# Modulation weights in tiles of their own, and their pieces moved in a two-layer trunk kernel

## The chip, the cores and the metric

The kernel runs on one core of a Trainium2 chip. The metric is the device time of one execution in microseconds (us); the kernel before takes 2713.36 us, the median of 3 runs (2710.75 to 2714.07).

## What is computed

The reference is two layers of a trunk for 640 tokens of width 1024 (128 context tokens and 512 latent ones), all in fp32. Each layer is a half-step FFN, a token mixer, and a second half-step FFN. The scale, shift and gate of each of the three come from one matrix product with the condition, the modulation ("adaLN"):

```python
def adaln(cond, w, b):
    m = (jax.nn.silu(cond) @ w + b).reshape(cond.shape[0], 1, N_MOD, D_MODEL)
    return [m[:, :, j] for j in range(N_MOD)]
...
def ffn_branch(x, mods, g_pre, g_post, w_in, w_out):
    shift, scale, gate = mods
    y = swiglu(modulate(x, g_pre, shift, scale), w_in, w_out)
    return x + FFN_RES * gate * rmsnorm(y, g_post)
...
    for i in range(DEPTH):
        m_ctx = adaln(c_ctx[None, :], mod_w[i], mod_b[i])
        m_lat = adaln(c, mod_w[i], mod_b[i])
        xc = ffn_branch(xc, m_ctx[0:3], norm_pre[i, 0], norm_post[i, 0], ffn_w_in[i, 0], ffn_w_out[i, 0])
...
        if i % 2 == 0:
...
            yc, s_ctx, ckv_ctx, krope_ctx = even_mixer(hc, *w, s0, None, None)
...
            yc, s_ctx = odd_mixer(hc, *w, s0)
```

The condition has two rows only (context and latent), but `mod_w` is 1024 x 9216 per layer: 75.5 MB for two layers, read once. The Even mixer (layer 0) is a gated DeltaNet with 4 heads (a chunked scan whose chunks need the inverse of a triangular matrix) beside an attention with 4 heads ("MLA"); the Odd mixer (layer 1) is a chunked gated linear attention. Two FFNs per layer have a hidden width of 2816.

## The kernel before

**Stages.** The program runs FFN1, Even mixer, FFN2 (layer 0), then FFN1, Odd mixer, FFN2 (layer 1), and stores. The 640 tokens are five tiles of 128. An FFN goes over 22 tiles of 128 hidden columns, t = 0 to 21: TensorE computes t's hidden columns (L650, 320 tokens wide), and the product with `w_out` (L298, 512 wide) of earlier tiles follows in between. Every product is taken as three products of a high and a low half of its operands. The halves of a weight are made on ScalarE (hi, L603 and L182) and VectorE (lo, L604 and L183) from a raw tile of 512 KB that SP's queue has loaded (L591, L196, L201). Behind an FFN's loop stand `half_a` and `half_b` (L810 to L822): the last output products, the norm, the gate and the residual for tiles 0 to 2, then for 3 and 4, and the next stage's normalisation and transposes (L257).

**Pools.** Tiles come from pools with a fixed number of buffers; an instruction that writes a tile waits until the tile that held its buffer has been read for the last time. Raw weights, the modulation weights `mw`, the modulation bias `mb` and the two gate tiles `gb` of a sub-layer all share the pool `rawp`, 7 buffers.

**Modulation.** `adaln` (L364) is a generator of 80 pieces, numbered 0 to 79 here: 2 layers x 5 column blocks x 8 slices of 128 rows (`kc`). A piece loads two `mw` tiles (blocks 0 to 3) or one (block 4) on SP's queue (L376). At every odd `kc` the matmuls of the last two pieces are issued (L395): a **flush**, with 8 matmuls of 32 x 512 over four column groups (16 records in the trace), or 4 matmuls over two groups in block 4 (8 records). After the eighth piece the bias is added (L403), the block is transposed (L407) and copied to `modF` (L413), or a gate is written to DRAM.

**Where pieces stand.** The program calls for a piece (`filler`) at places that tables set: FILLS gives for each FFN how many pieces stand in its loop (one per t, L802) and how many in `half_b` (L821); the Even mixer has calls behind its projections, two `self.fill(2)` (L1606, L1612), and MFILL, a count for each of the seven steps of each of four attention heads (L1595). In the Even mixer `mla_head(0)` runs together with what the scheduler can place beside it: `gdn_inverse(1)` (L1191), `gdn_levels` (L1225) and `gdn_chain(1)` (L1299) of the second pair of DeltaNet heads, mostly VectorE and ScalarE work with 128-wide matmuls between. Pieces 30 to 60 fall into the Even mixer, 61 to 70 into the loop of layer 0's FFN2, 71 to 76 into its `half_b`, and 77 to 79 into the loop of layer 1's FFN1.

**Order.** A scheduler at build time orders the instructions of each engine and gives out the buffers; at run time each engine and SP's queue goes through its list strictly in that order. A matmul of a flush whose `mw` has not landed holds up all of TensorE, and a load whose buffer is not free holds up all loads behind it.

Of the kernel before, what the change touches and what calls it, by code (L numbers as in the profile page):

```python
# [9 lines left out]
F32 = mybir.dt.float32  # L10
# [4 lines left out]
ALU = mybir.AluOpType  # L15
# [3 lines left out]
P = 128  # L19
# [3 lines left out]
KC = 8  # L23
# [4 lines left out]
HW = (6400, 4096)  # L28
HT = TOK // 2
PLAIN = 2  # L30
FILLS = (((16, 6), (10, 6)), ((18, 0), (0, 0)))
EARLY = 5
SLOTS = ((2, 3, 4, 5, 6), (0, 1, 2, 3, 4))
TW = 648
MFILL = ((1, 1, 1, 1, 1, 1, 0), (1, 1, 1, 1, 1, 1, 0), (1, 0, 1, 0, 1, 0, 0), (0, 0, 0, 0, 0, 0, 0))
NH = 4
KQ = 4
GLA_LEVELS = (1, 2, 4, 8, 16, 32, 64)
# [32 lines left out]
class Ring:  # L71


    def __init__(self, bufs):
        self.bufs, self.n = list(bufs), 0
# [6 lines left out]
class Trunk:  # L82
    def __init__(self, ctx, tc, cf, cm):
        self.tc, self.nc, self.n = tc, tc.nc, 0
        nc = self.nc
        mk = lambda name, bufs, **k: ctx.enter_context(tc.tile_pool(name=name, bufs=bufs, **k))
        self.cst = mk("cst", 1)
        self.hp = mk("hp", 1)
        self.xp = mk("xp", 5)
        self.rawp = mk("rawp", 7)  # L90
        self.hlp = mk("hlp", 16)
        self.Tp = mk("Tp", 18)
        self.sml = mk("sml", 2)
        self.ps_up = mk("ps_up", 3, space=PSUM)
        self.ps_dn = mk("ps_dn", 2, space=PSUM)
        self.ps_pt = mk("ps_pt", 2, space=PSUM)
        self.ps_ad = mk("ps_ad", 1, space=PSUM)
        self.dram = mk("drm", 1, space=bass.MemoryType.DRAM)
        self.ident = self.cst.tile([P, P], F32, name="ident")
        make_identity(nc, self.ident)  # L100
        self.ones = self.cst.tile([P, P], F32, name="ones")
        nc.vector.memset(self.ones, 1.0)
        self.mhalf = self.cst.tile([P, 1], F32, name="mhalf")
        nc.vector.memset(self.mhalf, -0.5)
        self.onec = self.cst.tile([P, 1], F32, name="onec")
        nc.vector.memset(self.onec, 1.0)
        self.cf = self.cst.tile([P, CTOT], F32, name="cf")
        self.cm = self.cst.tile([P, 8, P], U8, name="cm")
        self.neg = self.cst.tile([P, 2, P], BF16, name="neg")
        self.cm_in, self.cf_in = cm, cf  # L110
        self.x = [None] * NT
        self.h = [None, None]
        self.look = False
# [232 lines left out]
    def cond_setup(self, c, c_ctx, norm_pre):  # L346
        nc = self.nc
        t = self.raw("crow")
        nc.sync.dma_start(t[0:8, 0:P], c_ctx.rearrange("(k p) -> k p", p=P))
        nc.sync.dma_start(t[8:16, 0:P], c[0].rearrange("(k p) -> k p", p=P))  # L350
        nc.sync.dma_start(t[64:112, 0:P], norm_pre.rearrange("l n (k p) -> (l n k) p", p=P))
        ps = self.pt()
        nc.tensor.transpose(ps[:, 0:16], t[0:16, 0:P], self.ident[0:16, 0:16])
        ps2 = self.pt()
        nc.tensor.transpose(ps2[:, 0:48], t[64:112, 0:P], self.ident[64:112, 64:112])
        self.cT = self.cst.tile([P, KC, 32], F32, name="cT")
        nc.vector.memset(self.cT, 0.0)
        nc.scalar.activation(self.cT[:, :, 0:2].rearrange("p k r -> p r k"), ps[:, 0:16].rearrange("p (r k) -> p r k", r=2), AF.Silu)
        self.gpre = self.cst.tile([P, 48], F32, name="gpre")
        nc.vector.tensor_copy(self.gpre, ps2[:, 0:48])  # L360
        self.modF = [self.cst.tile([P, 9, 2, KC], F32, name=f"modF{l}") for l in range(2)]
        self.gate_dr = [[self.dram.tile([2, D], F32, name=f"gate{l}_{n}") for n in range(3)] for l in range(2)]

    def adaln(self, mod_w, mod_b, norm_post):  # L364


        nc = self.nc
# [3 lines left out]
        def load():  # L371
            for l, q, kc in order:
                wt = []
                for half in range(2 if q < 4 else 1):
                    w = self.W(name="mw") if (l, q) == (0, 0) else self.raw("mw")
                    nc.sync.dma_start(w, mod_w[l, kc * P:(kc + 1) * P, q * 2048 + half * 1024:q * 2048 + half * 1024 + 1024])  # L376
                    wt.append(w)
                ready.append(wt)
                return

        for l in range(2):
            for q in range(5):
# [25 lines left out]
                for mi in range(nj // 2):  # L408
                    n = 2 * q + mi
                    if n % 3 < 2:  # L410
                        for r in range(2):
                            src = pt.rearrange("p (c m j r) -> p c m j r", c=4, m=2, j=2)[:, :, mi, :, r]
                            nc.vector.tensor_copy(self.modF[l][:, n, r].rearrange("p (j c) -> p c j", c=4), src)  # L413
                    else:
                        o = 64 * mi
                        g = norm_post[l, n // 3]
                        nc.scalar.dma_start(mb[o:o + 64, 512:1024], bass.AP(g.tensor, g.offset, [[512, 2], [0, 32], [1, 512]]))
                        nc.vector.scalar_tensor_tensor(mb[o:o + 64, 0:512], mb[o:o + 64, 0:512], 1.0 if n // 3 == 1 else 0.5, mb[o:o + 64, 512:1024], ALU.mult, ALU.mult)
                        for j in range(2):
                            nc.scalar.dma_start(self.gate_dr[l][n // 3][:, j * 512:j * 512 + 512], mb[o + 32 * j:o + 32 * j + 2, 0:512])  # L420
                yield True

    def scale_shift(self, l, n):
        nc = self.nc
        A = self.cst.tile([P, 2, KC], F32, name=f"A{l}_{n}")
        g = self.gpre[:, (l * 3 + n) * 8:(l * 3 + n) * 8 + 8]
        for s in range(2):
            nc.vector.scalar_tensor_tensor(A[:, s], self.modF[l][:, 3 * n + 1, s], 1.0, g, ALU.add, ALU.mult)
        return A, self.modF[l][:, 3 * n]

    def gate_rows(self, l, n):
        out = []
# [460 lines left out]
class Even(Mixer):  # L893
# [87 lines left out]
    def run(self, nxt):  # L981
        T, nc, i = self.T, self.T.nc, self.i
# [3 lines left out]
        k, q, vtok, vpad = ([None] * NH for _ in range(4))  # L986
# [204 lines left out]
        def gdn_inverse(pair, st, ering):  # L1191
# [27 lines left out]
            for s in range(4):  # L1219
# [2 lines left out]
                    nc.vector.tensor_copy(U3[r, :, 32 * s:32 * s + 32], u3[r, u0:u0 + n])  # L1222
                for c in range(NT):
                    nc.scalar.copy(v4(st.D[c])[r, :, 32 * s:32 * s + 32], d3[r, 4 * c:4 * c + 4])
        def gdn_levels(st):  # L1225
            for lv in (4, 5):
                mask = T.cm[:, lv].unsqueeze(1).to_broadcast([P, 4, P])
                for c in range(NT):
                    a, uu, dd = st.A[c], st.U[c], st.D[c]
                    py, pz = misc(), misc()  # L1230
                    for u in range(4):
                        nc.tensor.matmul(un(py, u), lhsT=un(a, u), rhs=un(dd, u), start=True, stop=True)
                    Y = ering()
# [10 lines left out]
            for c in range(NT):  # L1244
                a, uu, dd = st.A[c], st.U[c], st.D[c]
                py, pz, Y = misc(), misc(), ering()
                for u in range(4):
                    r, k = where[u % 2]
# [4 lines left out]
                for u in range(4):  # L1253
                    r, k = where[u % 2]
# [44 lines left out]
        def gdn_chain(pair, st):  # L1299
# [28 lines left out]
                        square(h, 0)  # L1328

            for t in range(4):  # L1330
                if t == 2:
                    context()
                cu = (1 + t, 4 - t)
# [136 lines left out]
        st1 = gdn_store(1)  # L1470
# [132 lines left out]
                        gens.remove(g)  # L1603

        one = (mb, hq, prs, pTs)
        self.fill(2)  # L1606
        mla_values()
        together(mla_head(0, *one))
        gdn_inverse(1, st1, ering)
        early = [gdn_out(0)]  # L1610
        gdn_levels(st1)
        self.fill(2)  # L1612
        gdn_chain(1, st1)
        w_out = i["ev_w_out"][0]
        ar = T.arena(1)
# [476 lines left out]
```

## Time and profile before

| | us |
|---|---|
| median of 3 runs | 2713.36 |
| the profiled execution, its time | 2716.26 |
| its span | 2714.5 |
| TensorE matmul busy (PE) | 2632.5 (97%) |
| TensorE weight loads busy (PEld) | 2331.2 (86%) |
| VectorE busy (DVE) | 1943.0 (72%) |
| ScalarE busy (ACT) | 1179.1 (43%) |
| mean DMA rate | 114 GB/s |

PE is the engine that multiplies, PEld its weight loads, which run beside the multiplying; matmuls overlap in their pipeline, so that the records of neighbours overlap too and PE shows as busy where it could have taken more. The steps of the next sections are read from stretches of the trace, given in us from the start of the span. In the profiled execution the Even mixer lies from about 500 to 1000, layer 0's FFN2 from there to about 1470, and layer 1's FFN1 behind it.

### The profile page before, as it was taken

The page shows a single profiled execution, that of the slowest core. Times are in us where ns is not written, and L with a number is a line of the kernel's source. Part 1 is how long each engine was busy: PE and PEld are TensorE (multiplying, and loading weights), DVE is VectorE, ACT ScalarE, POOL GpSimd, SP SyncE. Part 2 cuts the span into 40 slices and gives each one's busy share as a digit, 9 for nine tenths or more (in the row PEclk, how much of TensorE's full clock was granted, in tenths as well). Part 3 has the DMA queues.
Part 4 walks back from the last instruction along what each step waited for, and adds up shares of the span by engine and source line. Part 5 has one row for each costly group of instructions (what it writes and reads, how often), then busy time and mean ns, then how long its engine had stood idle before and what let it go on. Part 6 is the DMA issues. An engine that isn't in the chain of part 4 may idle for free. (4 is left out here: it accounts for less than half of the span.)

```text
span 2714.5 us, 41232 instructions
## 1 busy us (share of the span) xinstructions
PE 2632.5 (97%) x16040; PEld 2331.2 (86%) x16040; DVE 1943.0 (72%) x3731; ACT 1179.1 (43%) x2281; POOL 125.5 (5%) x301
## 2 busy tenths in 40 slices
PE   6999999999999999999999999999999999999998
PEld 4988888789858678888997999999899988999997
DVE  5777777768585558777778777777675749777776
ACT  5433333554345645332335433334765447333333
POOL 0000000200100010000001000000200002000001
PEclk8999999999999999999999999999999999999999
DMA  8334424734151334343227322224212143332222
GB/s 272 123 115 141 148 96 133 251 103 142 50 188 46 128 117 130 114 138 103 86 71 244 104 87 86 86 81 135 92 55 67 59 140 109 95 92 86 78 70 101
DMA packets 297099, 309.60 MB, mean 114 GB/s; under 512 B 13573, under 2 KB 250639, under 8 KB 296903
## 3 DMA queue, kind: packets, MB, share of 16 engines
q1 hardware_dynamic: 278240, 260.05, 30.1%
q10 hardware_dynamic: 18663, 46.92, 4.9%
q8 instruction: 126, 2.06, 0.3%
q14 instruction: 70, 0.57, 0.1%
HBM read 286.59 MB, written 20.33 MB: 113 GB/s over the span
## 5 line engine op out<-in xcount | busy, mean ns | idle before, releaser
L650 PE MATMUL up<-ar,hi 128*128 128x320 f32 x2944 | 658.6, 311 | 10.5 <-ACT ar L513 4.5
L650 PEld LDWEIGHTS up<-ar,hi 128*128 128x128 f32 x2944 | 502.4, 189 | 37.2 <-ACT ar L513 6.1
L650 PE MATMUL up<-ar,lo 128*128 128x320 f32 x1472 | 455.5, 310 | 0.6 <-DVE lo L604 0.6
L603 ACT CAST hi<-raw 128x1024 fp32r<-128x1024 f32 x256 | 268.1, 1050 | 295.4 <-PE up L650 258.4
L304 DVE TENSOR_TENSOR y<-y,dn 128x512 f32<-128x512 f32 x388 | 264.5, 682 | 151.9 <-PE dn L298 150.8
L604 DVE TENSOR_TENSOR lo<-raw,hi 128x1024 fp32r<-128x1024 f32 x256 | 312.4, 1222 | 75.1 <-ACT hi L603 74.5
L298 PE MATMUL dn<-hi,al 128*128 128x512 f32 x880 | 347.8, 395 | 0.1
L298 PE MATMUL dn<-lo,ah 128*128 128x512 f32 x880 | 347.6, 395 | 0.0
L298 PE MATMUL dn<-hi,ah 128*128 128x512 f32 x880 | 346.8, 395 | 0.7 <-DVE y L304 0.5
L650 PE MATMUL up<-hq,hi 128*128 128x320 f32 x1408 | 315.1, 310 | 0.3 <-DVE xn L707 0.3
L650 PEld LDWEIGHTS up<-ar,lo 128*128 128x128 f32 x1472 | 277.9, 189 | 1.3 <-DVE lo L604 1.3
L208 PE MATMUL up<-ar,hi 128*128 128x384 f32 (+1 forms) x1184 | 267.3, 315 | 4.9 <-ACT ar L274 4.0
L650 PEld LDWEIGHTS up<-hq,hi 128*128 128x128 f32 x1408 | 238.8, 188 | 21.5 <-issue 9.2
L650 PE MATMUL up<-hq,lo 128*128 128x320 f32 x704 | 217.4, 309 | 0.0
L208 PEld LDWEIGHTS up<-ar,hi 128*128 128x128 f32 x1184 | 200.6, 191 | 15.3 <-issue 5.6
L183 DVE TENSOR_TENSOR lo<-raw,hi 128x1024 fp32r<-128x1024 f32 x145 | 175.8, 1218 | 45.0 <-ACT hi L182 38.2
L298 PEld LDWEIGHTS dn<-hi,al 128*128 128x128 f32 x880 | 165.3, 188 | 39.3 <-DVE al L691 1.2
L298 PEld LDWEIGHTS dn<-hi,ah 128*128 128x128 f32 x880 | 165.2, 188 | 26.3 <-DVE y L304 1.4
L208 PE MATMUL up<-ar,lo 128*128 128x384 f32 (+1 forms) x592 | 184.3, 311 | 0.0
L298 PEld LDWEIGHTS dn<-lo,ah 128*128 128x128 f32 x880 | 165.1, 188 | 22.2
L182 ACT CAST hi<-raw 128x1024 fp32r<-128x1024 f32 x145 | 150.9, 1048 | 44.5 <-PE up L208 19.0
L658 ACT COPY h<-up 128x320 f32<-128x320 f32 x68 | 29.0, 426 | 314.3 <-PE up L650 314.3
(704 smaller groups left out, 4216.2 us busy)
## 6 DMA issues: line engine op xcount, KB each, us to landing
raw<-in_ffn_w_in_dram SPq DMA_DIRECT2D x188, 512.0 KB
mw<-in_mod_w_dram SPq DMA_DIRECT2D x144, 512.0 KB
raw<-in_ffn_w_out_dram SPq DMA_DIRECT2D x88, 512.0 KB
xdr<-x ACTq DMA_DIRECT2D x25, 512.0 KB
x<-xdr ACTq DMA_DIRECT2D x25, 512.0 KB
raw<-in_od_w_in_dram SPq DMA_DIRECT2D x24, 512.0 KB
raw<-in_ev_w_in_dram SPq DMA_DIRECT2D x19, 512.0 KB
gb<-gate ACTq DMA_DIRECT2D x12, 512.0 KB
```

The lines of the kernel that those rows point to most:

```text
L182: nc.scalar.copy(hi, raw)
L183: nc.vector.tensor_sub(lo, raw, hi.bitcast(F32))
L208: self.nc.tensor.matmul(ps[:, :n], lhsT=wt[a][:, kc], rhs=self.h[g][:, b, kc], start=k == 0, stop=k == 3 * KC - 1)
L298: nc.tensor.matmul(ps, lhsT=a(i, m), rhs=w[j][:, nh * 512:nh * 512 + 512], start=k == 0, stop=k == last)
L304: nc.vector.tensor_add(yd, yd, ps)
L603: nc.scalar.copy(hi, raw[:, :n])
L604: nc.vector.tensor_sub(lo, raw[:, :n], hi.bitcast(F32))
L650: nc.tensor.matmul(ps[:, :HT], lhsT=w[i][:, kc], rhs=b[j].at(kc), start=first and n == 0, stop=n == 11, skip_group_check=not first)
L658: self.T.nc.scalar.copy(p1, X[:, :HT])
```

## The change

It does five things. `mw` tiles get a pool of 4 buffers, and `rawp` goes from 7 to 4. FILLS moves the six pieces of `half_b` behind layer 0's FFN2 into its loop. MFILL of attention head 0 goes from 6 pieces to 3, and the two `fill(2)` go; in their place `gdn_levels` of the second pair takes one piece at odd c (4 pieces), and each of the two `gdn_chain` one at t = 0 and 2 (4 pieces). `modF` keeps 6 rows in place of 9. A DMA scratch area shrinks from 1024 to 256 bytes. Pieces 30 to 61 now fall into the Even mixer, 62 to 77 into the loop of FFN2, none into its `half_b`, and 78 and 79 into the next loop.

```diff
-FILLS = (((16, 6), (10, 6)), ((18, 0), (0, 0)))
+FILLS = (((16, 6), (16, 0)), ((18, 0), (0, 0)))
...
-MFILL = ((1, 1, 1, 1, 1, 1, 0), (1, 1, 1, 1, 1, 1, 0), (1, 0, 1, 0, 1, 0, 0), (0, 0, 0, 0, 0, 0, 0))
+MFILL = ((1, 0, 1, 0, 1, 0, 0), (1, 1, 1, 1, 1, 1, 0), (1, 0, 1, 0, 1, 0, 0), (0, 0, 0, 0, 0, 0, 0))
...
-        self.rawp = mk("rawp", 7)
+        self.rawp = mk("rawp", 4)
+        self.mwp = mk("mwp", 4)
...
-        self.modF = [self.cst.tile([P, 9, 2, KC], F32, name=f"modF{l}") for l in range(2)]
+        self.modF = [self.cst.tile([P, 6, 2, KC], F32, name=f"modF{l}") for l in range(2)]
...
-                    w = self.W(name="mw") if (l, q) == (0, 0) else self.raw("mw")
+                    w = self.W(name="mw") if (l, q) == (0, 0) else self.mwp.tile([P, 1024], F32, tag="mw", name=self.u("mw"))
...
-        def gdn_levels(st):
+        def gdn_levels(st, fill=0):
...
                     py, pz = misc(), misc()
+                    if c % 2:
+                        self.fill(fill)
...
             for t in range(4):
+                if t % 2 == 0:
+                    self.fill(1)
                 if t == 2:
                     context()
...
         one = (mb, hq, prs, pTs)
-        self.fill(2)
         mla_values()
         together(mla_head(0, *one))
         gdn_inverse(1, st1, ering)
         early = [gdn_out(0)]
-        gdn_levels(st1)
-        self.fill(2)
+        gdn_levels(st1, 1)
         gdn_chain(1, st1)
...
-    nc = bacc.Bacc("TRN2", target_bir_lowering=False, num_devices=1, dynamic_dma_scratch_size=1024)
+    nc = bacc.Bacc("TRN2", target_bir_lowering=False, num_devices=1, dynamic_dma_scratch_size=256)
```

**TensorE behind layer 0's FFN2.** The first matmuls of the next FFN (L650, L651 after the change, since lines shift by one) and the flushes around them; `up` and `dn` are the products' accumulators, `ad` that of the modulation. Before:

```order
L257 MATMUL pt_13622<-ident,xn_13603 128x128 x4
L395 MATMUL ad_10645<-mw_13695,cT 32x512
L395 MATMUL ad_10645<-mw_13697,cT 32x512 x2
L650 MATMUL up_13862<-ar_13346,hi_13495 128x320
L650 MATMUL up_13888<-ar_13346,hi_13501 128x320
L650 MATMUL up_13862<-ar_13346,hi_13495 128x320
L650 MATMUL up_13862<-ar_13346,lo_13496 128x320
L407 MATMUL pt_13710<-ident,mb_13707 128x128 x4
L395 MATMUL ad_13719<-mw_13720,cT 32x512 x2
L395 MATMUL ad_13719<-mw_13722,cT 32x512 x2
L395 MATMUL ad_13719<-mw_13728,cT 32x512 x2
L395 MATMUL ad_13719<-mw_13730,cT 32x512 x2
```

With the change:

```order
L258 MATMUL pt_13674<-ident,xn_13655 128x128 x4
L299 MATMUL dn_13733<-hi_13323,al_13300 128x512
L396 MATMUL ad_11923<-mw_14419,cT 32x512
L396 MATMUL ad_11923<-mw_14571,cT 32x512 x2
L651 MATMUL up_13871<-ar_13398,hi_13547 128x320
L651 MATMUL up_13897<-ar_13398,hi_13553 128x320
L651 MATMUL up_13924<-ar_13398,hi_13559 128x320
L651 MATMUL up_13871<-ar_13398,hi_13547 128x320
L651 MATMUL up_13871<-ar_13398,lo_13548 128x320
```

The transposes and the two flushes that stood behind the first four matmuls of the next FFN are gone; the last flush of all (pieces 78 and 79), which the program calls for in the next loop, has been placed ahead of them, and that loop holds none any more.

**TensorE in the Even mixer.** Attention head 0 before, its scores, transposes and products with the values (L1546, L1568, L1575, L1579, L1584), with flushes in pieces between them:

```order
L1546 MATMUL up_6648<-kr_6645,hq_7267 128x320
L395 MATMUL ad_7524<-mw_8241,cT 32x512
L1584 MATMUL up_6647<-ident,pr_7268 128x128
L395 MATMUL ad_7524<-mw_8241,cT 32x512
L395 MATMUL ad_7524<-mw_8243,cT 32x512 x2
L1568 MATMUL up_6647<-ident,pr_7269 128x128 x4
L395 MATMUL ad_7524<-mw_8270,cT 32x512
L1575 MATMUL up_6648<-ident,pr_7269 128x128
```

With the change flushes stand in `gdn_levels` of the second pair (L1235 to L1242):

```order
L1239 MATMUL dn_4821<-ar_7163,E_5418 128x128 x4
L396 MATMUL ad_7775<-mw_7721,cT 32x512
L1242 MATMUL pt_4824<-ident,ar_7163 128x128 x4
L1239 MATMUL pt_4823<-ar_7163,E_5419 128x128 x4
L1235 MATMUL pt_4824<-ar_7164,ar_7163 128x128 x4
L1242 MATMUL dn_4822<-ident,ar_7163 128x128 x4
L396 MATMUL ad_7775<-mw_7721,cT 32x512
L396 MATMUL ad_7775<-mw_7723,cT 32x512 x2
L396 MATMUL ad_7775<-mw_7776,cT 32x512
```

Flushes that stood between the steps of the attention head now stand between the level products, three of them by the end of the levels.

**SP's queue between layer 0's FFN1 and the Even mixer.** `ev_w_in` is the mixer's projection weight. Before:

```order
L376 DMA mw_4667<-in_mod_w_dram 128x1024
L376 DMA mw_4669<-in_mod_w_dram 128x1024
L376 DMA mw_4671<-in_mod_w_dram 128x1024
L376 DMA mw_4673<-in_mod_w_dram 128x1024
L376 DMA mw_4683<-in_mod_w_dram 128x1024
L376 DMA mw_4685<-in_mod_w_dram 128x1024
L376 DMA mw_4687<-in_mod_w_dram 128x1024
L376 DMA mw_4689<-in_mod_w_dram 128x1024
L196 DMA raw_4837<-in_ev_w_in_dram 128x8x128
L196 DMA raw_4843<-in_ev_w_in_dram 128x8x128
L196 DMA raw_4966<-in_ev_w_in_dram 128x8x128
```

With the change:

```order
L197 DMA raw_4840<-in_ev_w_in_dram 128x8x128
L197 DMA raw_4846<-in_ev_w_in_dram 128x8x128
L197 DMA raw_4969<-in_ev_w_in_dram 128x8x128
L197 DMA raw_5039<-in_ev_w_in_dram 128x8x128
L197 DMA raw_5109<-in_ev_w_in_dram 128x8x128
L377 DMA mw_4670<-in_mod_w_dram 128x1024
L377 DMA mw_4672<-in_mod_w_dram 128x1024
L377 DMA mw_4674<-in_mod_w_dram 128x1024
L377 DMA mw_4676<-in_mod_w_dram 128x1024
L377 DMA mw_4686<-in_mod_w_dram 128x1024
```

The eight `mw` loads of the second and third flush there now stand behind five loads of projection weights, and each waits until TensorE has used up a tile of the flush before.

## Rows read from the trace of the kernel before

**Rows 1.** The page: span, busy time of each engine.

```profile
span 2714.5 us, 41232 instructions
PE 2632.5 (97%) x16040; PEld 2331.2 (86%) x16040; DVE 1943.0 (72%) x3731; ACT 1179.1 (43%) x2281; POOL 125.5 (5%) x301
```

**Rows 2.** Windows: stretch, its length, busy us (records) of each engine, clock, DMA share, GB/s.

```profile
510.00:530.00 20.00, 18.36 (x96) 11.03 (x92) 10.39 (x20) 9.27 (x22) 4.08 (x15) 1.00 1.06 358
785.00:815.00 30.00, 27.90 (x154) 15.04 (x152) 25.37 (x138) 14.70 (x39) 0.00 (x0) 1.00 0.65 235
815.00:850.00 35.00, 34.33 (x260) 30.17 (x259) 16.16 (x33) 21.19 (x57) 0.00 (x0) 1.00 0.09 34
1100.00:1430.00 330.00, 329.94 (x1970) 300.17 (x1970) 247.88 (x371) 109.70 (x151) 0.00 (x0) 1.00 0.34 107
```

**Rows 3.** Timeline of PE in FFN2's loop: start, length, instruction.

```profile
1112.22 1.92 PE L395 MATMUL ad<-mw,cT 128*32 128x512 f32 x16
1114.08 0.56 PE L650 MATMUL up<-hq,hi 128*128 128x320 f32 x2
```

**Rows 4.** Timeline of PE behind FFN2, [idle before <- what ended it].

```profile
1458.23 1.90 PE L395 MATMUL ad<-mw,cT 128*32 128x512 f32 x10
...
1467.60 1.06 PE L395 MATMUL ad<-mw,cT 128*32 128x512 f32 x6
1470.94 0.81 PE L650 MATMUL up<-ar,hi 128*128 128x320 f32 x3 [2.29 <-ACT ar L513]
1472.58 5.32 PE L395 MATMUL ad<-mw,cT 128*32 128x512 f32 x16
1477.83 0.56 PE L650 MATMUL up<-ar,hi 128*128 128x320 f32 x2
```

**Rows 5.** Timeline of DVE there: the last operand of the next FFN's first half.

```profile
1472.53 0.49 DVE L514 TENSOR_TENSOR ar<-f,ar 128x192 fp32r<-128x192 f32 x2
```

**Rows 6.** Timeline of SP there.

```profile
1459.32 10.16 SPq L376 DMA_DIRECT2D mw<-in_mod_w_dram  x5
1472.68 8.14 SPq L591 DMA_DIRECT2D raw<-in_ffn_w_in_dram  x5
```

**Rows 7.** Timeline of PE in layer 1's FFN1.

```profile
1498.54 1.04 PE L395 MATMUL ad<-mw,cT 128*32 128x512 f32 x2
...
1534.88 1.90 PE L395 MATMUL ad<-mw,cT 128*32 128x512 f32 x6
1536.71 0.56 PE L650 MATMUL up<-hq,hi 128*128 128x320 f32 x2
...
1570.20 1.91 PE L395 MATMUL ad<-mw,cT 128*32 128x512 f32 x8
```

**Rows 8.** Windows of line 395 alone: busy us (records) of PE and PEld.

```profile
785.00:815.00 30.00, 9.51 (x48) 1.34 (x48) 1.00 0.65 235
815.00:850.00 35.00, 0.00 (x0) 0.00 (x0) 1.00 0.09 34
```

**Rows 9.** DVE's waits from 765 to 960: us in total, times, longest.

```profile
DVE mx L1547 <- PE up L1546: 10.4, 13, 1.4
```

**Rows 10.** SP's waits over the whole span.

```profile
SPq L591 <- DVE lo L604: 701.0, 85, 32.4
SPq L376 <- PE ad L395: 221.7, 32, 29.0
```

**Rows 11.** Timeline of PE between FFN1 and the Even mixer.

```profile
507.50 2.78 PE L395 MATMUL ad<-mw,cT 128*32 128x512 f32 x24
...
512.09 1.05 PE L395 MATMUL ad<-mw,cT 128*32 128x512 f32 x4
...
524.14 0.44 PE L257 MATMUL pt<-ident,xn 128*128 128x128 f32 x2 [1.24 <-ACT h L239]
```

**Rows 12.** Timeline of SP there.

```profile
512.11 15.09 SPq L196 DMA_DIRECT2D raw<-in_ev_w_in_dram  x6
```

**Rows 13.** Timeline of DVE there: the last product with a gate tile.

```profile
510.01 0.68 DVE L281 TENSOR_TENSOR y<-y,gb 128x512 f32<-128x512 f32 x1
```

More of the change, by code (lines that the diff above doesn't have):

```diff
@@ L412, in adaln @@
                             src = pt.rearrange("p (c m j r) -> p c m j r", c=4, m=2, j=2)[:, :, mi, :, r]
-                            nc.vector.tensor_copy(self.modF[l][:, n, r].rearrange("p (j c) -> p c j", c=4), src)
+                            nc.vector.tensor_copy(self.modF[l][:, n - n // 3, r].rearrange("p (j c) -> p c j", c=4), src)
                     else:
@@ L427, in scale_shift @@
         for s in range(2):
-            nc.vector.scalar_tensor_tensor(A[:, s], self.modF[l][:, 3 * n + 1, s], 1.0, g, ALU.add, ALU.mult)
-        return A, self.modF[l][:, 3 * n]
+            nc.vector.scalar_tensor_tensor(A[:, s], self.modF[l][:, 2 * n + 1, s], 1.0, g, ALU.add, ALU.mult)
+        return A, self.modF[l][:, 2 * n]
     def gate_rows(self, l, n):
```

## The prediction

> **What bounds the kernel.** I read the page first, then the windows, then the timelines at the places that the diff touches. The page shows TensorE busy for 2632.5 of 2714.5 us and nothing else above 72% [rows 1]; so a change pays only where TensorE waits, or where it does work that could be done in a wait. The windows tell the two kinds of place apart. In the loop of layer 0's FFN2 PE is busy for 329.94 of 330 us and its weight loads for 300.17 [rows 2]: there is no wait, and whatever is put in is paid in full. In the Even mixer from 785 to 815, with attention head 0, PE shows 27.90 of 30 but PEld only 15.04, while DVE has 25.37: matmul records overlap there without the array being full, VectorE sets the pace, and a matmul put between costs little. From 815 to 850, where the second pair's chain follows, PEld is at 30.17 of 35 and DVE at 16.16 [rows 2]: PE is nearly full again. The same 80 pieces are computed before and after; the change only moves 40 flushes about. The reader is to see that it moves some from places where PE waits to places where it does not, and others the other way.
>
> **The price of a flush.** In the FFN2 loop a flush of 16 records begins at 1112.22 and the next matmul at 1114.08: 1.86 us [rows 3]. In layer 1's FFN1 a flush of 8 records, two column groups in place of four, takes from 1534.88 to 1536.71: 1.83 us [rows 7]. So half the work costs the same, and I take 1.85 us for either kind where PE is saturated.
>
> **Term 1, the loop of layer 0's FFN2.** Before, four flushes stand there, up to piece 69; with the change seven, up to piece 77. Three more at 1.85 us in a stretch without idle time: **+5.6 us**. A flush there has no cover, so below 5 us it can't be.
>
> **Term 2, behind layer 0's FFN2.** Three flushes stood here. The first was in two parts: one, of 1.90 us, stood among the output products at 1458.23, and I take 1.8 us for it; the other, at 1467.60, lies in a wait of 2.29 us that ends only when ScalarE has the next FFN's operand at 1470.94, and costs nothing [rows 4]. The other two came as 16 records of 5.32 us at 1472.58, and the next matmul of the FFN starts at 1477.83 [rows 4]. What these matmuls need was there when VectorE ended the last `ar` at 1472.53 + 0.49 = 1473.0 [rows 5], so 4.8 us of this are delay. They took 5.3 us in place of 3.7 in a stretch where SP issued five `mw` loads over 10 us and the next weights only from 1472.68 [rows 6], so part was waiting for data. All of it goes: 1.8 + 4.8 = **-6.6 us**. The bound on the other side: if the next weights are late once this delay is gone (they are issued at 1472.68 now), only the 1.8 us stay. I take nearly the whole, because SP no longer has `mw` loads ahead of those weights and the first tile's weights are split before 1473. The last flush (pieces 78, 79) now stands right ahead of the next FFN's first matmul, in the place of the one at 1467.60: the wait of 2.29 us hides it, 0 to +1.9 us; I take **0**.
>
> **Term 3, layer 1's FFN1.** The two flushes that stood in its loop (2 + 6 and 8 records) go: 0.97 us for the small part (1498.54 to about 1499.5), 1.83 and, for the 8 records of 1.91 us at 1570.20, 1.84 [rows 7]: **-4.6 us**, in a loop as full as FFN2's.
>
> **Term 4, the Even mixer.** It takes one flush more. From 785 to 815 48 records of L395, three flushes, lay between attention head 0's steps, and from 815 to 850 none [rows 8]. With the change three stand in the second pair's levels, where PE is nearly full, so up to 3 x 1.85 = 5.6 us that were hidden come out, and the added flush may cost 1.85 more: at most +7.4. Against it, VectorE waited 10.4 us for scores of attention over the heads [rows 9], and flushes ahead of those scores are part of that; with half of head 0's pieces gone some of it returns: -4 us at best. From the weight-load share I take 50% of the exposed 5.6 us, 2.8, and of the added one 0.5, less 2: **+1.3 us**, with -4 and +7.4 as ends. Here a rule speaks against the move. The Trainium skill ("Trainium Kernel Development and Optimization", Best Practices) says to judge how near TensorE is to its limit by the busy share of its weight loads and not of its matmuls; by matmul share head 0 (93%) and the levels (98%) look alike and term 4 would be only the added flush, about +2; by the weight loads (50% and 86%) head 0 has room and the levels don't, and it would be up to +7. No row decides it; the rows of VectorE make me stay between.
>
> **Term 5, the pools.** Four raw buffers in place of seven: in an FFN a t needs three raw loads, and SP already spent 701 us waiting for buffers of that kind [rows 10], which cost PE nothing in the saturated loops; I take 0 there. Two gate tiles hold two of the four at each stage's end, where the next weights may come later by the 3 us of two tiles at 358 GB/s [rows 2]: 0 to +3 us; **+0.5**. The `mw` pool of four is just one flush: the next flush's loads wait for PE to use up the last, and PE releases them already in 221.7 us of waits now [rows 10]. That matters only where flushes follow closely, between FFN1 and the Even mixer, where a flush and a half run at 507.50 and the next parts from 512.09 on [rows 11]. There the next four tiles can no longer be loaded early, but their place in the transfers goes to projection weights, which before were issued from 512.11 on [rows 12], and the stretch from 510 to 530 moved 358 GB/s at a DMA share of 1.06 [rows 2]: total bytes bound it, and these are the same. 0 to +7 (worked out below), **+1**.
>
> The smaller `modF` and scratch area change no instruction: 0. I know of no row in which a DMA needs that area.
>
> **The sum.** 5.6 - 6.6 - 4.6 + 1.3 + 0.5 + 1 = -2.8. Against the profiled execution, 2716.3, this gives 2713.5; that execution lies 2.9 above the median of 2713.4, so against the runs it is 2710.6. Predicted: **2710.5 us**. About 0.2%, 5.4 us, is what a measurement of this kernel can tell from no change: below 2708.0 is faster, above 2718.8 slower.
>
> **The rivals.**
> *A, the mixer gains (faster).* If VectorE's chain of head 0 and the inverse beside it is what ends the mixer's middle, and the flushes moved into the levels fill short waits of PE there for ScalarE and VectorE, term 4 is -4 and not +1.3: 2705. For it: DVE at 25.37 of 30 us and the 10.4 us of waits [rows 2, 9]. Against it: 30.17 of 35 us of weight loads in the levels' stretch.
> *B, `mw` starves (slower).* Between FFN1 and the mixer the four tiles of the next flush are behind five projection loads in SP's queue, and the last of these waits for a buffer that a gate tile holds until its last product ends at 510.69 [rows 13]. Then the first `mw` is issued near 511 and four tiles of 0.52 MB land at 358 GB/s, 1.46 us each, by 517 and later, plus a projection tile ahead of them; PE, which wanted the first of them within the flushes of 507.50 to 510.28 [rows 11], stands for 5 to 7 us, and a second time for the flush behind, of 2 to 3. This decides if that last buffer comes free later than about 509. Some of it falls in waits that are there anyway (1.24 us at 524.14 [rows 11]; PEld is at 11.03 of 20 [rows 2]). Net +8 in place of +1, and with an exposed mixer (+3 to +7) it gives 2719 to 2724, slower than before.
> *C, the change brings nothing.* The moved flushes cost in FFN2's loop what they gain behind it, the weights behind it are late so that only 1.8 of 6.6 us come, and the rest is as summed: 2715.
>
> **How the numbers follow.** The forecast, within 4 us of its sum, 0.45; A 0.2; B 0.2; C 0.15. The sum's own spread is some 4 us, so about two fifths of the forecast lie below 2708.0 and none above 2718.8; all of A below; most of B above, C within. Faster 0.18 + 0.2 = 0.38; slower 0.2, with a little for what I have not seen 0.22; same 0.40. The range from 2700 (A with a full gain behind FFN2) to 2722 (B) leaves out 0.2.
>
> **What would show it.** In the changed kernel: the loop of FFN2 longer by 5 to 6 us from its first L651 to its last; no L396 between the next FFN's first matmuls, and that FFN's second half reached some 6 us sooner after FFN2's end; layer 1's FFN1 without any L396. In the mixer, the stretch of the levels longer by 2 to 5 us and head 0 shorter by as much or less. PE waits of over 1 us on `mw` loads behind FFN1 would show B. The forecast is wrong if the mixer as a whole moves by more than 5 us either way, if the gain behind FFN2 comes back as a wait for raw weights a few us on, or if PE waits for `raw` in an FFN loop.

## The result, and the profile after

The changed kernel takes **2729.03 us** (median of 4, 2728.18 to 2730.27) against 2713.72 us for the kernel before on the same chip (median of 4): 15.3 us more, a ratio of 1.0057 with a 95% interval of 1.0045 to 1.0070. The forecast was 2710.5 us, with a range of 2700 to 2722.

The page of the kernel after, span and busy times, beside [rows 1]:

```profile
span 2726.2 us, 41151 instructions
PE 2648.7 (97%) x16040; PEld 2338.6 (86%) x16040; DVE 1941.0 (71%) x3731; ACT 1179.0 (43%) x2281; POOL 132.0 (5%) x301
```

TensorE executes as many instructions as before, and is busy 16 us longer with them. To see where, each matmul record of a source line was paired with the record of the same line and the same number in the trace before; the median of the differences of their starts, over the matmuls that in the trace before began in the 25 us from the time given on (10 us in the mixer and at 1492), is the **lag** of the kernel after. It was computed from the two traces:

```
matmuls that began before at   lag, us   what lies there
 225                            +0.7     layer 0's FFN1
 475                            -4.6     end of FFN1
 525                            -1.3     first projections of the Even mixer
 675                            -2.2     end of the projections
 780                            -2.5     start of attention head 0
 830                            +6.8     levels of the second pair
 870                           +11.2     its chain
 950                           +16.0     attention heads 2 and 3
1180                           +16.2     layer 0's FFN2, ahead of the added flushes
1400                           +22.3     its end
1492                           +16.2     next FFN, first tile
1575                           +14.2     next FFN
2700                           +11.7     end
```

In these two executions the lag at the end is 11.7 us, while the medians are 15.3 apart; the execution profiled before was 2.5 us slower than the median of its four runs, the one after 0.8 us faster. The table shows FFN2 and the part behind it close to the forecast, and one stretch with a loss of 18 us: the Even mixer from 780 to 950. Half of it, 9.3 us, comes up to 830, with attention head 0, and half, 9.2, behind it. Windows of the kernel after there, with the columns of [rows 2]:

```profile
785.00:790.00 5.00, 4.84 (x16) 3.21 (x14) 3.29 (x25) 1.03 (x3) 0.00 (x0) 0.64 0.30 122
795.00:800.00 5.00, 4.33 (x13) 2.71 (x12) 2.12 (x14) 2.06 (x6) 0.00 (x0) 0.50 0.00 0
800.00:805.00 5.00, 4.64 (x21) 4.00 (x21) 3.58 (x23) 0.63 (x2) 0.00 (x0) 0.65 0.00 0
785.00:815.00 30.00, 24.67 (x87) 17.69 (x85) 20.12 (x128) 10.77 (x30) 0.00 (x0) 0.66 0.05 21
815.00:850.00 35.00, 34.14 (x239) 25.16 (x239) 15.71 (x37) 17.57 (x49) 0.00 (x0) 1.00 0.37 121
```

The third number from the right is the granted clock: 0.66 over head 0's stretch, with 0.50, the lower of TensorE's two levels (1.2 in place of 2.4 GHz), from 795 to 800, where [rows 2] has 1.00. PE issued 87 matmuls there in place of 154. The windows of the flushes alone show what left and where it went; first after (L396), then before (L395):

```profile
785.00:825.00 40.00, 0.00 (x0) 0.00 (x0) 0.74 0.04 16
825.00:860.00 35.00, 9.51 (x48) 1.34 (x48) 1.00 0.46 151
```

```profile
785.00:825.00 40.00, 9.51 (x48) 1.34 (x48) 1.00 0.55 199
825.00:860.00 35.00, 1.04 (x2) 0.14 (x2) 1.00 0.05 17
```

The same 48 records, three flushes, moved as a block from attention head 0 to the levels. What PE did just before the clock fell, and how the flushes stand in the levels now (timeline of PE, kernel after):

```profile
781.17 1.06 PE L396 MATMUL ad<-mw,cT 128*32 128x512 f32 x6
784.52 0.39 PE L1551 MATMUL up<-hq 128*128 128x256 f32 x1 [2.30 <-ACT hq L1505]
...
825.69 1.05 PE L396 MATMUL ad<-mw,cT 128*32 128x512 f32 x2
826.66 0.66 PE L1242 MATMUL pt<-ident,ar 128*128 128x128 f32 x4
...
829.62 1.07 PE L396 MATMUL ad<-mw,cT 128*32 128x512 f32 x8
830.62 1.16 PE L1239 MATMUL dn<-ar,E 128*128 128x128 f32 x8
...
833.19 1.06 PE L396 MATMUL ad<-mw,cT 128*32 128x512 f32 x6
834.18 0.91 PE L1537 MATMUL up<-ckv,ukv 128*128 128x384 f32 x2
```

PE waited 2.30 us, and a stretch of attention with few matmuls follows. In the levels one flush of 16 records comes in three runs of 2, 8 and 6 records; each delays the next matmul by about 1.0 us (826.66 - 825.69, 830.62 - 829.62, 834.18 - 833.19), 2.96 us for the flush, whatever the number of records, while an unbroken one costs 1.86 [rows 3]. Three of them are 8.9 us. Behind 830 the granted clock is 1.00 (815 to 860 in the windows above, and on to 1000), so the second half of the loss arises at the full clock. VectorE's waits from 765 to 970 answer to [rows 9]:

```profile
DVE mx L1552 <- PE up L1551: 17.8, 15, 2.1
```

VectorE now waits 17.8 us for scores, where it waited 10.4: the opposite of the relief that was forecast.

### The profile page after: what moved, and what is told of

It reads as the page before. It is cut to its first block, busy times and chain, and to the rows that moved or that the text cites. A ratio compares the mean times of both kernels' runs of the same rounds, so it can differ in the third digit from the quotient of the medians.

```text
span 2726.2 us, 41151 instructions
## 1 busy us (share of the span) xinstructions
PE 2648.7 (97%) x16040; PEld 2338.6 (86%) x16040; DVE 1941.0 (71%) x3731; ACT 1179.0 (43%) x2281; POOL 132.0 (5%) x301
## 4 chain that ended last, share of the span: by engine, by line
PE 56%; issue 33%; DVE 4%; ACT 2%; POOL 2%; DMA 2%; ACTq 0%; SPq 0%; POOLq 0%; DVEq 0%
PE up L651 18%; PE dn L299 13%; PE up L209 9%; PE ad L396 3%; PE up L1837 2%; PE dn L1817 1%; PE up L1551 1%; POOL rstd L232 1%; POOL ss L224 1%; PE up L1584 1%; PE pt L258 1%; POOL rstd L231 1%; DMA mw<-in_mod_w_dram 1%; DMA cf<-const_cf_dram 0%; ACT junk L219 0%
## 5 line engine op out<-in xcount | busy, mean ns | idle before, releaser
L651 PE MATMUL up<-ar,hi 128*128 128x320 f32 x2944 | 659.0, 311 | 8.2 <-ACT ar L514 3.5
L651 PEld LDWEIGHTS up<-ar,hi 128*128 128x128 f32 x2944 | 502.0, 189 | 35.4 <-ACT ar L514 5.1
L651 PE MATMUL up<-ar,lo 128*128 128x320 f32 x1472 | 455.4, 310 | 0.1
L651 PE MATMUL up<-hq,hi 128*128 128x320 f32 x1408 | 314.9, 310 | 0.0
L651 PEld LDWEIGHTS up<-ar,lo 128*128 128x128 f32 x1472 | 277.9, 189 | 0.8 <-DVE lo L605 0.8
L651 PEld LDWEIGHTS up<-hq,hi 128*128 128x128 f32 x1408 | 238.5, 188 | 22.6 <-issue 12.6
L651 PE MATMUL up<-hq,lo 128*128 128x320 f32 x704 | 217.2, 309 | 0.0
L209 PEld LDWEIGHTS up<-ar,hi 128*128 128x128 f32 x1184 | 200.6, 191 | 18.5 <-issue 12.9
L651 PE MATMUL up<-hq,hilo 128*128 128x320 f32 x960 | 154.3, 309 | 0.0
```

What stands on the lines that cost most here:

```text
L209: self.nc.tensor.matmul(ps[:, :n], lhsT=wt[a][:, kc], rhs=self.h[g][:, b, kc], start=k == 0, stop=k == 3 * KC - 1)
L651: nc.tensor.matmul(ps[:, :HT], lhsT=w[i][:, kc], rhs=b[j].at(kc), start=first and n == 0, stop=n == 11, skip_group_check=not first)
```

## The experiments

The kernel before was run again beside each set, with medians of 2713.1 to 2713.4 us.

**1 and 2. The fill places or the pools?** The first takes the changed kernel and puts the mixer's fill places back; the second takes the kernel before and makes only the change of places.

```diff
-MFILL = ((1, 0, 1, 0, 1, 0, 0),
+MFILL = ((1, 1, 1, 1, 1, 1, 0),
...
-                if t % 2 == 0:
-                    self.fill(1)
...
         one = (mb, hq, prs, pTs)
+        self.fill(2)
...
-        gdn_levels(st1, 1)
+        gdn_levels(st1)
+        self.fill(2)
```

Expected of the mixer put back:

> The changed kernel with only the Even mixer's fill places put back (six pieces in attention head 0, the two fill(2), none in the levels and chains); the pools of 4 and 4 and the 16 pieces in FFN2's loop stay. Theory P (places): the whole loss lies in the mixer between 785 and 890, because the pieces left attention head 0 (TensorE's granted clock there 0.50 to 0.69) and went into the levels; this kernel then takes about 2729 - 18 = 2711 us, the mixer's head 0 shows a clock of 1.00, and FFN2's loop and the part behind it stay at +6 and -8 us. Theory Q (pools): the mw tiles of 4 delay the pieces wherever they stand; then at least 8 of the 16 us stay, 2720 us or more.

Expected of the places alone (the change's own edit of them, in the kernel before):

> The kernel before, with its shared pool of 7 and its old FILLS, and only the Even mixer's fill places of the change. Theory P: the loss is there without the pools: about 2714 + 14 to 18 = 2728 to 2732 us, with the clock below 0.8 between 785 and 815. Theory Q: the seven shared buffers let the pieces be loaded early, and it stays within 5 us of before, 2709 to 2719 us.

Measured: mixer put back **2712.66 us** (ratio to before 0.9995, 0.9985 to 1.0004), places alone **2732.64 us** (1.0072, 1.0057 to 1.0087). Windows of both, mixer put back first:

```profile
785.00:815.00 30.00, 29.09 (x157) 14.56 (x152) 25.36 (x120) 13.30 (x36) 0.00 (x0) 1.00 0.68 219
```

```profile
785.00:815.00 30.00, 24.22 (x95) 17.83 (x93) 21.72 (x139) 12.05 (x35) 0.00 (x0) 0.72 0.00 1
```

The places alone cost 19 us, with seven shared buffers and the old FFN tables; without them the rest of the change is worth nothing measurable. Theory Q falls: the loss comes with the fill places and goes with them. So does the clock: 1.00 with six pieces in head 0, 0.72 with three.

**3. Six pieces in head 0 again, the levels kept.** Edit in the changed kernel: the first row of MFILL back to (1, 1, 1, 1, 1, 1, 0).

> The changed kernel with six pieces in attention head 0 in place of three, the pieces in the levels and chains kept. Clock theory: flushes between head 0's steps keep TensorE's clock at 1.00 there, so that stretch becomes 5 to 7 us shorter although it holds more work, and the levels keep most of their cost: 2719 to 2724 us. Without a part of the clock (only the flushes' own time in the levels counts): head 0's stretch gets no shorter and the time stays at 2727 to 2731 us.

Measured: **2724.92 us** (1.0038, 1.0023 to 1.0053).

```profile
785.00:815.00 30.00, 29.38 (x154) 15.53 (x154) 24.12 (x155) 12.94 (x37) 0.00 (x0) 1.00 0.68 240
```

With more matmuls in the stretch the clock held 1.00, and the lag grew by 3.1 us from 780 to 830, not by 9.3 as in the changed kernel. But the gain did not last: from 830 to 960 the lag grew by 20.5 us here (1.8 to 22.3) and by 9.2 in the changed kernel (6.8 to 16.0); the clock was 0.83 again from 860 to 870 and 0.86 from 900 to 910. The program has one and a half flushes more in the mixer, and more of them came late: the trace has 330 records of L396 between 480 and 1010, against 288, and 54 behind that, against 96. So the total, 4.1 us below the changed kernel's, goes with fewer flushes behind the mixer, and this run does not show that the clock of head 0 shortens the mixer as a whole. The total lies 0.9 us above the range of the clock theory.

**4. No piece called for in the levels.** Edit: `gdn_levels(st1, 1)` back to `gdn_levels(st1)`.

> The changed kernel without the four pieces in the levels (three in attention head 0, four in the chains kept; the pieces left over go on to the FFN loops). Theory P with two parts, the clock in head 0 and flushes that stand in the levels, each in three runs of about 1 us: the levels get 6 to 8 us shorter, head 0 keeps its low clock, and two flushes more in FFN loops cost 3.7 us: 2723 to 2727 us. If the levels' flushes cost nothing beside the clock: 2729 us or more.

Measured: **2723.72 us** (1.0039, 1.0024 to 1.0054). The granted clock from 785 to 815 was 0.66 again and the lag grew by 9.0 us from 780 to 830, as in the changed kernel; from 830 to 870 it grew by 3.1 us, not by 4.4, and from there to 960 by 2.9, not by 4.8. The window, and PE's flush records up to 850:

```profile
785.00:815.00 30.00, 24.94 (x87) 17.97 (x87) 20.21 (x130) 10.17 (x30) 0.00 (x0) 0.66 0.09 33
```

```profile
838.71 1.04 PE L396 MATMUL ad<-mw,cT 128*32 128x512 f32 x2
842.26 1.06 PE L396 MATMUL ad<-mw,cT 128*32 128x512 f32 x8
845.83 1.06 PE L396 MATMUL ad<-mw,cT 128*32 128x512 f32 x6
```

One flush still stands among the level products, placed there from another call; two of the three have left. These two were worth about 3 us of the mixer's 18, half of the 5.9 us that their runs add up to in the trace of the changed kernel. What the third costs, and the four pieces in the chains, no run takes out alone; the rest of the loss behind 830 stays open.

**5 to 8. Is it the clock?** A flush in head 0 may help in two ways: its own work is hidden, and it keeps the clock up. Useless matmuls, into columns that nobody reads, do only the second. The first kernel:

```diff
+                    if h == 0:
+                        for _ in range(6):
+                            nc.tensor.matmul(ps[:, 320:512], lhsT=qn[0][m], rhs=kn[0][:, 0:192], start=True, stop=True)
```

> The changed kernel with useless matmuls in attention head 0: six of 128x192 ahead of each of its nine score products, into columns of the accumulator that nobody reads, some 54 x 0.1 = 5 to 6 us of TensorE work at full clock. Clock theory: they keep the granted clock at or near 1.00 between 785 and 815, and the time falls by 0 to 6 us although work was added: 2723 to 2729 us. If the clock is of no account: the added work comes on top of a chain that waits for scores, 2731 to 2735 us.

Measured: **2730.42 us** (1.0061, 1.0046 to 1.0076).

```profile
785.00:815.00 30.00, 24.30 (x110) 19.50 (x110) 25.88 (x141) 12.02 (x42) 0.00 (x0) 0.72 0.09 33
```

The useless matmuls needed the same operands as the scores and so stood behind the same wait; this run settled nothing. The next three put them on an operand that is ready early, ahead of each score product (`first`) and between a transpose and the product that waits for its copy (`second`); their numbers are 4 and 10 (heavy), 1 and 4 (light), and 1 and 4 with 4 ahead of the first three products (front):

```diff
+                    if h == 0:
+                        for _ in range(4 if m < 2 else 1):
+                            nc.tensor.matmul(ps[:, 320:512], lhsT=V[0][:, 0:P], rhs=V[0][:, 0:192], start=True, stop=True)
...
+                if h == 0:
+                    for _ in range(4):
+                        nc.tensor.matmul(pb[:, 3 * P:4 * P], lhsT=V[0][:, 0:P], rhs=V[0][:, 0:P], start=True, stop=True)
```

Heavy:

> The changed kernel with useless matmuls in attention head 0, on operands that are ready early: four of 128x192 ahead of each score product and ten of 128x128 between a transpose and the product that waits for its copy, some 10 us of TensorE work at full clock. In the first such run the clock fell all the same, behind a wait of 3.75 us that no useless matmul filled. Clock theory: the granted clock stays at 0.95 or more from 785 to 815, and the time is that of the changed kernel or less, 2723 to 2730 us, although 10 us of work were added. If the clock is of no account: 2733 us or more.

Light:

> The changed kernel with fewer useless matmuls in attention head 0 than the run with some 19 us of them (they took twice the time I had put down): one of 128x192 ahead of each of nine score products (0.39 us each) and four of 128x128 in each of five steps (0.96 us), 8 us in all. In the heavy run the clock held 1.00 and the stretch from 775 to 825 took no longer than in the changed kernel, 19 us of work for nothing. Clock theory: the clock holds 0.95 or more again, and the same matmuls of the mixer reach 825 some 2 to 6 us earlier than in the changed kernel. If the clock is of no account, they come later there by about the added 8 us less the waits they fill, 0 to 5 us. If so few do not hold the clock, the run tells nothing on it.

Front:

> The changed kernel with the useless matmuls of the light run and three more ahead of each of the first three score products, where TensorE waits for VectorE before 785 and after which the clock still fell to 0.65 for 10 us in the light run (0.89 over 785 to 815): some 12 us of work. Clock theory: the clock holds 1.00 from 785 on, and from 780 to 830 the matmuls fall behind those of before by 3 to 7 us, against 9.3 in the changed kernel and 6.1 in the light run, with more work than either. If the clock is of no account: by 10 us or more.

Measured: heavy **2735.6 us** (1.0081, 1.0066 to 1.0096), light **2726.83** (1.0052, 1.0038 to 1.0066), front **2726.56** (1.0049, 1.0033 to 1.0064). Windows of heavy, light and front, in this order:

```profile
785.00:815.00 30.00, 29.18 (x188) 24.50 (x187) 26.16 (x145) 13.01 (x45) 0.00 (x0) 1.00 0.11 36
```

```profile
785.00:815.00 30.00, 25.73 (x135) 19.57 (x135) 24.66 (x143) 12.56 (x34) 0.00 (x0) 0.89 0.11 36
```

```profile
785.00:815.00 30.00, 25.91 (x156) 20.33 (x156) 26.68 (x148) 13.47 (x40) 0.00 (x0) 1.00 0.11 36
```

The useless work and the growth of the lag from 780 to 830, against the granted clock from 785 to 815 (the work is the number of useless records by the time of one run of them at full clock):

```
kernel                     useless work, us   clock   lag grows by, us
changed kernel                    0           0.66        9.3
places alone                      0           0.72        7.7
first useless run                 8           0.72       10.6
light                             7.5         0.89        6.1
front                            10.5         1.00        6.5
heavy                            23           1.00       10.8
six real pieces in head 0         0           1.00        3.1
mixer put back                    0           1.00        0.9
```

The first useless run and the light one do about the same amount of useless work; the one with the clock at 0.89 falls behind by 4.5 us less. That alone is no proof, since in the first run the useless matmuls stand behind the wait of the scores and in the light one they fill waits. But with 10.5 us of useless work and the full clock the lag grows by less than in the changed kernel with none (6.5 against 9.3 us), which the added work alone does not explain. The heavy run had 23 us and not the 10 that I had expected, since each fp32 matmul is two records; its total of 2735.6 met the number of the theory without the clock, but with 23 us of added work its stretch fell behind by only 1.5 us more than the changed kernel's. So the clock costs some us there, at least the 3 or so that light and front win back; how many exactly can't be read off, because useless matmuls also stand in the way of real ones. From 780 to 950 the lag grows by 16.3 us in light and 15.9 in front, by 18.5 in the changed kernel. The totals of light and front lie 2 us below the changed kernel's, with intervals that overlap: it is the stretch that shows the clock, not the totals.

**9. The pools alone.** Edit in the kernel before: `rawp` 4, `mwp` 4, nothing else of the change that moves work.

> The kernel before with only the pools changed (4 raw buffers and 4 of mw's own); the tables as before. From the run with the mixer put back, pools and FFN2 tables together give 2712.7 against 2713.3. If the six pieces moved into FFN2's loop give the -5.7 us that were summed, the pools alone cost 4 to 6 us: 2717 to 2720. If the pools cost nothing, the six pieces give nothing either: 2712 to 2715.

Measured: **2717.32 us** (1.0017, 1.0007 to 1.0027). The pools alone cost 4 us, and the tables then give 4.7 (2712.66 against 2717.32). Where PE waits in the mixer of this run, 700 to 970:

```profile
PE ad L396 <- DMA mw<-in_mod_w_dram: 2.3, 3, 1.1
```

Its lag grows by 4.5 us between 750 and 780 and by 3.8 near 900. Four buffers are one flush, and the next can only be loaded behind it; the waits for `mw` that the trace shows are 2.3 us of this, and the rest was not traced to its cause.

**10. The FFN2 table alone**, in the kernel before: `(16, 6), (10, 6)` to `(16, 6), (16, 0)`.

> The kernel before with one number pair changed: the six pieces behind layer 0's FFN2 go into its loop; shared pool of 7 and the mixer's places as before. The run with the pools alone took 2717.3 and that with pools and these tables 2712.7, so the tables gave 4.6 us there. If that gain does not need the pools, this kernel takes 2713.2 - 4.6 = 2708 to 2710 us and is the fastest so far. If behind FFN2 the next weights wait for the shared buffers, it stays at 2712 or more.

Measured: **2716.77 us** (1.0015, 1.0006 to 1.0024), slower. PE behind FFN2 in this run (timeline):

```profile
1474.03 1.17 PE L650 MATMUL up<-ar,hi 128*128 128x320 f32 x3 [4.07 <-ACT ar L513]
1475.00 0.47 PE L650 MATMUL up<-ar,lo 128*128 128x320 f32 x1
1475.27 0.73 PE L650 MATMUL up<-ar,hi 128*128 128x320 f32 x2
```

Nothing stands in the wait for ScalarE any more: it is 4.07 us long, and behind it the matmuls run at half pace (the one behind 1475.00 starts 0.27 us later, where at full clock, in the changed kernel, such starts lie 0.14 us apart, at 1493.09 and 1493.23); the window from 1470 to 1480 has a granted clock of 0.67. As in head 0, the clock is low where no flush is left. The lag falls by 3.1 us here (1400 to 1492), less than the 6.5 that the three flushes add to the loop. The weights were not late; that part of the expectation was wrong.

**11. More pieces in heads 2 and 3**, on top of the mixer put back: their rows of MFILL to (1, 1, 1, 1, 1, 1, 0) and (1, 0, 1, 0, 1, 0, 0).

> The run with the mixer put back, with five pieces more in attention heads 2 and 3 (MFILL of head 2 six, of head 3 three), so that FFN2's loop and the next FFN hold about two and a half flushes fewer, 4.6 us. If heads 2 and 3 have room for them: 2707 to 2710 us. If they are as full as the levels: 2712 us or more.

Measured: **2722.64 us** (1.0040, 1.0025 to 1.0055), 10 us more than without. The lag grows by 13 us from 880 to 960. Weight loads take only 28.35 of 45 us there (29.57 without the added pieces, second line):

```profile
905.00:950.00 45.00, 45.00 (x243) 28.35 (x241) 23.08 (x70) 23.74 (x63) 0.00 (x0) 1.00 0.43 151
905.00:950.00 45.00, 45.00 (x256) 29.57 (x255) 25.47 (x80) 27.84 (x74) 0.00 (x0) 1.00 0.35 114
```

A low share of weight loads was no room for a flush here: PE's matmuls are busy for all 45 us in both runs, and a flush counts little in that share (48 records take 9.51 us of PE and 1.34 of its weight loads [rows 8]). Two heads run together there, and each score stands in PE's order behind whatever flush is ahead of it; that this is what costs the 10 us is likely and not shown.

**12. Eight shared buffers.** The run with the mixer put back, its 4 and 4 buffers as one pool.

```diff
-        self.rawp = mk("rawp", 4)
-        self.mwp = mk("mwp", 4)
+        self.rawp = mk("rawp", 8)
...
-                    w = self.W(name="mw") if (l, q) == (0, 0) else self.mwp.tile([P, 1024], F32, tag="mw", name=self.u("mw"))
+                    w = self.W(name="mw") if (l, q) == (0, 0) else self.raw("mw")
```

> The run with the mixer put back, but its 8 buffers (4 raw, 4 mw) as one shared pool of 8; 16 pieces in FFN2's loop. So far: shared 7 with the old tables 2713.4, shared 7 with 16 pieces in the loop 2716.8, own 4 and 4 with the old tables 2717.3, own with 16 pieces 2712.7. If the gain behind FFN2 needs mw tiles that no gate or weight tile can hold up, 8 shared buffers do no better than 7: 2714 to 2718 us, and the matmuls behind FFN2 gain about 3.5 us against before, not 8. If the eighth buffer is what helped: 2711 us or less, with some 8 us gained there.

Measured: **2708.36 us** (0.9984, 0.9976 to 0.9993): the fastest of all, 5 us below before and 21 below the changed kernel. The gain is not where it was expected: behind FFN2 the lag falls by 4.0 us, little more than with seven buffers. It falls by 6.0 us in FFN1 between 225 and 475 against 0.3 in run 10, part of it the wait of PE for VectorE's sum of the bias (L403), 3.2 us from 240 to 475 in the trace of before and gone here; and by 3 us in the mixer, where run 10 had 0. The gain in FFN1 goes with eight buffers in place of seven and not with sharing them: with 4 and 4 it is 5.3 us too, in run 9 and in the changed kernel. What sets sharing apart is the mixer, where the lag of run 1 grew by 5.2 us from 675 to 950.

## Why the prediction was wrong

- **Term 4 failed, and it alone decided.** "+1.3 us, with -4 and +7.4 as ends" was +18 (lag from -2.2 at 675 to +16.0 at 950), and runs 1 and 2 show that the fill places cost it. Both ends were prices of flushes at full clock; that the flushes in head 0 also kept TensorE's clock up was in no term. Taking them out was to cost nothing there and to win up to 4 us; head 0's stretch fell behind by 9.3 us in place of that, at a clock of 0.66, and by 3.1 with six pieces and 1.00 (run 3). How much of the whole is the clock's was not shown: light and front, with useless work of their own, won back 3 us in the stretch and 2 to 3 by 950, and in run 3 nothing was left of the gain by 960. Of the 9.2 us behind 830, at full clock, about 3 are two flushes in the levels (run 4); the cause of the others stays open. The rows read were enough to ask: PE's weight loads were busy for half of head 0's stretch [rows 2], and the pieces were a third of its records, 48 of 154 [rows 2, 8]; [rows 2] show the clock at 1.00 *with* them. The Trainium skill ("TensorE: Matmul & The Clock Gate", Why this matters for your kernels) says to leave no long idle gaps between runs of matmuls if the clock is not to drop. The trace agrees in direction, with 1.00 before and 0.66 after in the stretch that lost its flushes.
- **The price of a moved flush** was taken as 1.85 us at most. Between the short steps of the levels the scheduler broke each into three runs of about 1.0 us, 2.96 together. That made the bound too low, though run 4 got only about 3 us back for two of them.
- **VectorE's 10.4 us of waits** [rows 9] were read as in part caused by flushes that would go. They grew to 17.8.
- **Term 1** was right: +5.6 forecast, +6.1 measured (lag +16.2 at 1180 to +22.3 at 1400).
- **Term 2** was right in size: -6.6 forecast, -6.1 measured (+22.3 to +16.2 at 1492). Run 10 shows why the last flush in that wait matters: with no flush left there the clock is low and only half the gain comes. But one reading in it was wrong. That the two flushes took 5.3 us in place of 3.7 was put down in part to waiting for data. In the trace of before PE waited there for ScalarE alone (2.29 us [rows 4]); then the clock fell, and records of a flush took up to 1061 ns in place of 592:

```profile
1470.00:1475.00 5.00, 3.93 (x16) 1.73 (x18) 4.84 (x17) 2.61 (x11) 1.06 (x3) 0.80 0.76 262
1475.00:1480.00 5.00, 5.00 (x26) 2.60 (x22) 3.07 (x7) 3.73 (x9) 0.94 (x4) 0.86 0.83 243
```

```profile
L395 PE MATMUL ad<-mw,cT x16: 592/838/1061, 1472.6 to 1477.3; 128*32 128x512 f32 x16
```

So the clock's price behind a wait of 2 us, some 1.6 us here, could have been read before the change.

- **Term 3** was right as to the flushes: the lag drops by 0.8, 2.0 and 2.0 us where they stood, 4.8 against 4.6. New waits of PE for ScalarE and the like in the same loop gave 2.8 back, so it ends at -2.0 (+16.2 to +14.2).
- **Term 5** was right in sign, and small at the place that it names: +3.3 us between FFN1 and the mixer (lag -4.6 to -1.3) against +1, within its 0 to +7. That is the place of rival B and less than half of its price of 8; a wait for `mw` of 1.2 us is in the trace there, and the rest was not traced. Run 9 shows what the term left out: with the old places the pools win 5.3 us in FFN1 (225 to 475) and lose 8.1 in the mixer (675 to 950), 4.2 net against the +1.5 of the term.
- **The rivals.** A had the mixer's sign wrong. B ended on the right side, at 2719 to 2724, in the wrong place. C was wrong in its reason: behind FFN2 the gain came nearly whole. Without term 4 the forecast's other terms sum to -4.1 and the lag outside the mixer to 11.7 - 18.2 = -6.5.

## What to carry to other kernels

Work that fills an engine's waits may be doing two jobs, as the flushes in head 0 did: it is hidden itself, and on TensorE it keeps the granted clock up for the chain that it hides behind. Before moving filler out of a stretch that is bound by other engines, ask what share of TensorE's records it is there, and read the clock of a stretch that has no filler. And count a piece of work by the runs in which the scheduler will place it: here each run between short matmuls delayed the next one by about 1 us, with 2, 6 or 8 records alike. Last, follow a stretch that was mended to the end of its stage: what head 0 won in run 3 was gone by the end of the mixer.

## What the hardware showed that was not expected

- The granted clock fell to 0.50 behind a PE wait of 2.30 us and a stretch with few matmuls, and the mean over 30 us was 0.66; behind FFN2 a wait of 4.07 us was followed by matmuls at half pace (run 10), and in the kernel before a wait of 2.29 us by a clock of 0.80 and 0.86.
- At the low clock the share of weight loads rises with less work: 17.69 us for 85 loads (0.208 us each) after, 15.04 us for 152 before [rows 2]. Of these, 48 are the short ones of flushes with 1.34 us in all [rows 8]; the other 104 took 0.132 us each. A higher share of weight loads was not a fuller TensorE but a slower one.
- Two column groups cost as much as four: 1.83 us for 8 records, 1.86 for 16 [rows 3, 7].
- Own buffers were worse than shared ones at the same size of memory: 4 and 4 gave 2712.66 us, 8 shared 2708.36.
